# A trunk layer's attention mixers: the second logit pass over all 128 rows, and a compressed branch padded to 128 keys

## The chip, the cores and the metric

The kernel runs on one core of a Trainium2 chip. The metric is the device time of one execution in microseconds; of the kernel before it is the median of three runs. Engines are named as in the profile: PE is TensorE (PEld its weight loads), DVE VectorE, ACT ScalarE, POOL GpSimd, SP the engine whose queue issues most loads.

## What is computed

The reference is one layer of a decoder on 1024 tokens of 1024 features, in float32. After a first norm, four attention mixers work side by side, each with heads of 64 features: A (sparse attention with a selected, a window and a compressed branch, 4 heads), B (dilated windows in three groups, 2 heads each), C (forgetting attention, 4 heads) and D (latent attention, 4 heads). Their outputs are projected, gated and merged, and a gated MLP with a short convolution follows. Of mixer A, cut to what matters:

```python
lc = einsum('bqhd,bcd->bhqc', q_blk, kc) * scale          # compressed: 63 keys
p_c, _ = masked_softmax(lc, cmp_end <= t)
o_c = einsum('bhqc,bcd->bqhd', p_c, vc)
...
ls = einsum('bqhd,bqkd->bhqk', q_blk, ks) * scale + bias   # selected: here all keys up to t
lw = einsum('bqhd,bkd->bhqk', q_blk, kw) * scale + bias    # window: the last 512 keys
...
return g0 * o_c + g1 * o_s + g2 * o_w
```

## The kernel before

**Precision by passes.** Float32 products run as sums of float32r products: an operand x is split into hi = float32r(x) and lo = x - hi, and hi*hi + lo*hi + hi*lo is accumulated in PSUM. A head has 64 features, half of TensorE's 128 rows, so mixers A, B and C stack the halves: `q_pair` (L320) makes for each head e of a pair a tile qs[e] with q's hi part on the 64 partitions 64e.. and its lo part on the other 64; `k_pair` (L327) makes ks[e] with k's hi part on both. One pass over 128 rows then gives hi*hi + lo*hi, and a second pass over 64 rows adds q's hi times kl, k's lo part. `q_passes` (L443) lists these two. For the pairs of C and B, kl is one tile in which head e has the partitions 64e..; for A, whose keys all heads share (`shared`), the lo part already stands on both halves, as it does in KCL, the lo part of the compressed keys KC. Mixer D has operands of 96 rows and three passes.

**One softmax row block** (`softmax_rows`, L361): the passes of up to 512 keys into PSUM (L374; for B's groups 1 and 2 L372), one VectorE instruction that adds the bias and takes the running maximum into a tile P (L376), exp on ScalarE (L381), and scaling by the row sum and the branch's gate on VectorE (`normalize`). `pv` (L394) takes key blocks of 128 in groups of at most two: it transposes P's blocks for two query blocks on TensorE (L413), splits them on ScalarE (th, L419) and VectorE (tl, L420), zeroes the blocks that are masked throughout on GpSimd (L417, L418), and multiplies with the value stack: th with all 128 columns [hi | lo] (L428, L431), tl with the 64 of hi (L429). `fold` adds the two halves.

**Stages.** In program order: the norm and token-major columns, A's compressed keys and values (KC, KCL, VC; L484 to L595), D (about 150 to 275 us of the profile), A (275 to 516), C (516 to 640), B's group 0 (640 to 692), the projections of B's groups 1 and 2 (to 743.7) and their attention (to about 790), then the merge, the output projection and the MLP. A runs over 4 heads and in each over 4 pairs of query blocks (g): selected, window, compressed, each with its own P tiles, into one PSUM tile pvt. Queries' 128-row blocks take 12 key chunks a head over all keys, and as many in the window.

**Order.** The order of each engine's instructions is planned at build time: an instruction goes into its engine's queue by program order and readiness in the plan, and the queue is then strictly in order. So projections (`project`, 48 products of 512 columns each, L142 to L144 on tile pd) of the next mixers stand between the attention's products. `fill_tile` (L191) computes gate products early (tile pf) at the lowest priority; its weights come in two halves through the tile fraw. Tiles of one tag share a ring of BUFS[tag] buffers.

Of the kernel before, what the change touches and what calls it, by code (L numbers as in the profile page):

```python
"""Hybrid decoder trunk (one layer) on one Trainium2 core.

Normalisations run token-major; products take their operands feature-major (features on
partitions, tokens on the free axis), so normalised activations are transposed on TensorE.
Float32 products run as three float32r passes: an operand x is split exactly into
hi = float32r(x) and lo = x - hi, and hi*hi + hi*lo + lo*hi is accumulated in PSUM.
"""
# [16 lines left out]
D = 1024  # L24
# [13 lines left out]
BUFS = dict(qs=4, ks=4, kl=3, vs=2, vt=1, P=4, th=2, tl=2, bias=2, ot=2, fo=2, nm=8, lsq=1)  # L38
# [10 lines left out]
def shape_constants():  # L49
    """Arrays that depend on shapes alone."""  # L50
    c = {}
    # distance rows: [0,1280) dist = 1023 - i; [1280,1791) dist = 4 * (255 - i); [1792,1919) dist = 16 * (63 - i)
# [24 lines left out]
    # [open | causal triangle | closed] and, for the window's far end, [closed | triangle | open]  # L77
# [8 lines left out]
def body(tc, a, out):  # L86
# [39 lines left out]
    def load_weights(src, shape, pool_=None, scale=1.0, eng=None):  # L126
        """DMA one weight tile and split it into float32r halves."""
        pool_ = pool_ or wp
        raw = wp.tile([128] + shape, F32, name="wraw", tag="wraw", bufs=2)
        SP.dma_start(raw, src)  # L130
        hi = pool_.tile([128] + shape, F32R, name="whi", tag="whi", bufs=2)
        lo = pool_.tile([128] + shape, F32R, name="wlo", tag="wlo", bufs=2)
        split_weights(hi, lo, raw, eng or V, scale)
        return hi, lo

    def gemm(ps, lhs, rhs, kts, first=True, last=True):
        """ps += lhs^T rhs in three passes; lhs(kt) and rhs(kt) give (hi, lo)."""
# [8 lines left out]
    def row_rstd(rs, sums):  # L146
        """rs = 1 / sqrt(sums / D + eps), one per partition."""
        A.activation(rs, sums, AF.Sqrt, bias=epst[:, 0:1], scale=1.0 / D)
        V.reciprocal(rs, rs)
# [6 lines left out]
    def to_features(src, psum, dst, b):  # L156
        """dst (hi, lo) [128, KT, 512], token block b = transpose of src [128 tokens, D], split."""
# [17 lines left out]
    # ================= token mixers =================  # L175
    with ExitStack() as c1:
# [13 lines left out]
        # ---- gates that need nothing but h: work for TensorE whenever the mixers wait  # L190
        def fill_tile(i):  # L191
            br, m = FILL[i]
            w = []
            for ch in range(2):
                raw = ap.tile([128, 4, 128], F32, name="fraw", tag="fraw", bufs=2)
# [20 lines left out]
        # ---- h = rms_norm(x) * gain by token blocks, transposed and split  # L216
        def weights_tm(src):
            """Weights of the token-major columns, in four pieces of two feature tiles."""
# [31 lines left out]
        # ================= token-major columns: latents, rotary key, gates, forget logits =================  # L250
# [19 lines left out]
        cmpmask = ap.tile([128, 8, 64], F32, name="cmpmask")  # L270
        SP.dma_start(cmpmask, a["cmpmask"])
# [12 lines left out]
        def toeplitz(row):  # L284
            """tile[p, j]: row value at distance p + 896 - j."""
# [4 lines left out]
        def project(src, scale=1.0):  # L290
            """Feature-major projection of h: yields (half, psum tile)."""
# [9 lines left out]
        def permuted(ap_, hf, kind):  # L301
            """Columns of tokens 512*hf.. in natural, (r4,s,i) or (r4,4i+s) order, as [p, r4, s, i]."""
# [9 lines left out]
        def split(hi, lo, ps, kind):  # L312
            """hi = float32r(ps), lo = ps - hi."""
# [13 lines left out]
        def k_pair(src, kind="n", shared=False):  # L327
            ks = [ap.tile([128, S], F32R, name="ks", tag="ks", bufs=BUFS["ks"]) for _ in range(2)]
            kl = [ap.tile([128, S], F32R, name="kl", tag="kl", bufs=BUFS["kl"]) for _ in range(2 if shared else 1)]
            for hf, ps in project(src):  # L330
                for e in range(2):
# [7 lines left out]
                    else:  # L339
                        lo_of(permuted(kl[0][64 * e:64 * e + 64], hf, kind),  # L340
                              permuted(ks[e][64 * e:64 * e + 64], hf, kind), pe, kind)
            return ks, (kl if shared else [kl[0], kl[0]])
# [17 lines left out]
        # ---- one softmax row block: logits in chunks, joint maximum, exp, sum  # L360
        def softmax_rows(chunks, clamp=BIG, stat=None, two=False):  # L361
            """chunks: (passes, n, bias). Returns P [128, sum n] = exp(l - max) and its row sums;
            -max and the sums go to the columns of stat if there are any."""
            P = ap.tile([128, S], F32, name="P", tag="P", bufs=BUFS["P"])
# [29 lines left out]
        def pv(pvt, P2, blocks, first, last):  # L394
            """pvt[hi 64 | lo 64, 256 queries] += V^T P^T over key blocks. A block: the column of its
            first key in P for either query block (None where it is masked throughout), rows, V stack."""
# [3 lines left out]
            for bl in groups:  # L400
                kr = bl[0][1]
                # slots in an order that leaves the ones to move in one piece
# [30 lines left out]
        def fold(dst, pvt, e):  # L433
            """dst (partitions 64e..) = sum of the two halves of pvt."""
# [8 lines left out]
        def q_passes(qs, e, ks, kl, qb, k0, n):  # L443
            q = slice(128 * qb, 128 * qb + 128)
            r = slice(64 * e, 64 * e + 64)
            return [(qs[:, q], ks[:, k0:k0 + n], 0), (qs[r, q], kl[r, k0:k0 + n], 0)]

        def cuts(k0, k1):
            """Key chunks: at most 512 columns, none under 256 unless it is the only one."""
# [10 lines left out]
        def causal_blocks(vs, k1):  # L460
            """Key blocks of query blocks k1 - 2 and k1 - 1, both from key 0 on."""
            return [((128 * b, 128 * b), 128, vs[:, b]) for b in range(k1 - 1)] + [
                ((None, 128 * (k1 - 1)), 128, vs[:, k1 - 1])]
# [4 lines left out]
        def rotate(x, n):  # L468
            """x [128, n blocks, heads, 32] rotated in place; n = (first block, blocks, heads)."""
# [13 lines left out]
        # ================= A, compressed keys and values =================  # L483
        KC = ap.tile([128, 64], F32R, name="KC")  # L484
        KCL = ap.tile([128, 64], F32R, name="KCL")
        VC = ap.tile([64, 128], F32R, name="VC")
# [13 lines left out]
        # the keys' and the values' columns apart, zeros elsewhere: one product serves both  # L500
# [7 lines left out]
        # rms-normalised latents, transposed, gained and split  # L508
# [5 lines left out]
        for i, (c0, n, dst, gc) in enumerate(kinds):  # L514
            for b in range(8):
                sq = ap.tile([128, 256], F32, name="lsq", tag="lsq", bufs=BUFS["lsq"])
# [27 lines left out]
        # gates of A  # L544
# [3 lines left out]
        # log sigmoid(f + bias) = min(z, 0) - ln(1 + exp(-|z|)), then its running sum over tokens  # L548
# [28 lines left out]
        # gelu(x) = 0.5 x (1 + tanh(sqrt(2/pi) (x + 0.044715 x^3)))  # L577
# [19 lines left out]
        # ---- bias rows (table lookup by one-hot product), then to DRAM for the Toeplitz reads  # L597
# [12 lines left out]
        # Row copies at a pitch one (or four) longer than the one they are read at: each partition  # L610
        # then reads its row one (or four) further on.
# [5 lines left out]
        # ================= D: latent attention =================  # L617
# [25 lines left out]
        # on the partitions where the keys' tiles take it  # L643
# [18 lines left out]
        for pr in range(2):  # L662
            QD, KD = [], []
            for e in range(2):
# [5 lines left out]
                else:  # L670
                    # the two operands of a subtraction start in the same quadrant
# [34 lines left out]
        # ================= A: native sparse attention =================  # L706
        # n_sel equals the number of selected blocks at this sequence length, so every block is
        # selected whatever its importance, and the selected branch is causal attention over all keys.
        ks, kl = k_pair(a["win"][1], shared=True)
        va = v_pair(a["win"][2])  # L710
        for pr in range(2):
            qs = q_pair(a["win"][3 + pr])
            ot = new_ot()
            for e in range(2):
# [3 lines left out]
                for g in range(4):  # L718
                    pvt = new_pv()
                    # selected  # L720
# [605 lines left out]
```

## Time and profile before

| | |
|---|---|
| median of three runs | 1940.14 us (1940.08 to 1941.3) |
| the profiled execution, its span | 1942.8 us |
| granted TensorE clock, mean over the span | 0.992 |
| instructions | 24124 |

The trace is of one execution; its span is the time from its first to its last instruction and the only time that the profile gives for it, 2.7 us over the median of the runs. Clock 1.00 is 2.4 GHz. Products on TensorE overlap: in a timeline the start of one and its length are shown, and the end of one less the end of the one before it is what it adds to the engine's time. A form such as 64*128 64x256 is a product over 64 rows into 128 columns of outputs, with 256 moving columns.

### The profile page before, as it was taken

The page shows a single profiled execution, that of the slowest core. Times are in us where ns is not written, and L with a number is a line of the kernel's source. Part 1 is how long each engine was busy: PE and PEld are TensorE (multiplying, and loading weights), DVE is VectorE, ACT ScalarE, POOL GpSimd, SP SyncE. Part 2 cuts the span into 40 slices and gives each one's busy share as a digit, 9 for nine tenths or more (in the row PEclk, how much of TensorE's full clock was granted, in tenths as well). Part 3 has the DMA queues.
Part 4 walks back from the last instruction along what each step waited for, and adds up shares of the span by engine and source line. Part 5 has one row for each costly group of instructions (what it writes and reads, how often), then busy time and mean ns, then how long its engine had stood idle before and what let it go on. Part 6 is the DMA issues. An engine that isn't in the chain of part 4 may idle for free.

```text
span 1942.8 us, 24124 instructions
## 1 busy us (share of the span) xinstructions
PE 1890.3 (97%) x8894; PEld 1506.2 (78%) x8894; DVE 1103.0 (57%) x2109; ACT 789.6 (41%) x1466; POOL 513.0 (26%) x510
## 2 busy tenths in 40 slices
PE   7989999999999999999999999999999999999998
PEld 6767777676777777788888888778888888888786
DVE  4449867877777525432222245679777766733534
ACT  5436545554555534221212134444444444432432
POOL 3411111120120220011222200567676767100000
PEclk9999999999999999999999999999999999999999
DMA  7150110000001110321122232212222222354643
GB/s 252 41 149 17 62 45 24 24 31 20 28 22 43 51 44 28 124 74 53 59 69 65 69 125 108 98 56 98 76 87 76 87 77 82 114 157 147 222 156 109
DMA packets 55366, 158.83 MB, mean 82 GB/s; under 512 B 9344, under 2 KB 10704, under 8 KB 55248
## 3 DMA queue, kind: packets, MB, share of 16 engines
q1 hardware_dynamic: 42352, 124.09, 19.9%
q10 hardware_dynamic: 12896, 33.21, 4.9%
q8 instruction: 70, 1.15, 0.2%
q14 instruction: 48, 0.39, 0.1%
HBM read 129.91 MB, written 31.61 MB: 83 GB/s over the span
## 4 chain that ended last, share of the span: by engine, by line
PE 89%; DVE 4%; ACT 2%; issue 2%; DMA 1%; POOL 1%; ACTq 0%; DVEq 0%; SPq 0%; POOLq 0%
PE ps L374 6%; PE pgb L142 6%; PE pgb L143 6%; PE pgb L144 5%; PE pd L143 4%; PE pd L142 4%; PE pd L144 4%; PE pk L1217 4%; PE pk L1219 4%; PE pk L1218 4%; PE ptp L413 4%; PE pvt L428 2%; PE pvt L429 2%; PE py L143 2%; PE py L142 2%; PE pz L143 2%
## 5 line engine op out<-in xcount | busy, mean ns | idle before, releaser
L142 PE MATMUL pgb<-hh,whi 128*128 128x512 f32 x400 | 155.8, 390 | 1.0 <-ACT ft L206 0.7
L144 PE MATMUL pgb<-hh,wlo 128*128 128x512 f32 x400 | 155.6, 389 | 0.0
L143 PE MATMUL pgb<-hl,whi 128*128 128x512 f32 x400 | 155.6, 389 | 0.0
L120 DVE TENSOR_TENSOR wlo<-wraw,whi 128x1024 fp32r<-128x1024 f32 x25 | 30.6, 1224 | 210.3 <-ACT whi L119 210.3
L419 ACT CAST th<-ptp 128x512 fp32r<-128x512 f32 (+3 forms) x202 | 97.7, 517 | 118.8 <-PE ptp L413 108.5
L381 ACT ACTIVATE P<-P,nm 128x64 f32<-128x64 f32 (+8 forms) x160 | 107.8, 675 | 82.7 <-DVE nm L376 81.7
L420 DVE TENSOR_TENSOR tl<-ptp,th 128x512 fp32r<-128x512 f32 (+3 forms) x202 | 115.2, 598 | 35.9 <-ACT th L419 33.5
L142 PE MATMUL pd<-hh,whi 128*128 128x512 f32 x320 | 133.4, 417 | 1.9 <-DVE kl L318 1.9
L119 ACT CAST whi<-wraw 128x1024 fp32r<-128x1024 f32 x38 | 39.9, 1051 | 234.4 <-PE pgb L143 196.0
L143 PE MATMUL pd<-hl,whi 128*128 128x512 f32 x320 | 133.2, 416 | 0.0
L144 PE MATMUL pd<-hh,wlo 128*128 128x512 f32 x320 | 132.7, 415 | 0.0
L1217 PE MATMUL pk<-aset 128*128 128x512 f32 x320 | 124.6, 390 | 0.6 <-DVE y L1257 0.6
L1218 PE MATMUL pk<-aset 128*128 128x512 f32 x320 | 124.5, 390 | 0.5 <-DVE aset L120 0.5
L1219 PE MATMUL pk<-aset 128*128 128x512 f32 x320 | 124.4, 390 | 0.0
L1084 POOL TENSOR_TENSOR aset<-sums,aset 128x512 fp32r<-128x512 f32 x66 | 121.5, 1841 | 6.4 <-ACT aset L1083 6.4
L417 POOL MEMSET th<- 128x128 f32 x86 | 18.2, 212 | 377.5 <-PE pvt L428 233.7
L972 POOL TENSOR_TENSOR mg<-mg,tg 128x512 f32<-128x512 f32 x32 | 42.1, 1317 | 286.9 <-DVE tg L970 241.6
L413 PE MATMUL ptp<-miscc,P 128*128 128x128 f32 (+1 forms) x678 | 110.8, 274 | 2.9 <-DVE P L390 2.3
L1083 ACT CAST aset<-wraw 128x512 fp32r<-128x512 f32 x88 | 54.0, 617 | 97.9 <-PE pz L144 37.7
L120 DVE TENSOR_TENSOR aset<-at,aset 128x512 fp32r<-128x512 f32 x44 | 30.3, 691 | 107.2 <-ACT aset L119 107.0
L413 PEld LDWEIGHTS ptp<-miscc,P 128*128 128x128 f32 (+1 forms) x678 | 80.3, 139 | 14.0 <-DVE P L390 4.3
L1083 ACT CAST aset<-sums 128x512 fp32r<-128x512 f32 x66 | 40.8, 620 | 120.7 <-PE px L144 29.0
(359 smaller groups left out, 5129.4 us busy)
## 6 DMA issues: line engine op xcount, KB each, us to landing
wraw<-in_wup SPq DMA_DIRECT2D x44, 512.0 KB, 3.6
wraw<-in_wdn SPq DMA_DIRECT2D x44, 512.0 KB, 3.5
wraw<-in_wg SPq DMA_DIRECT2D x25, 512.0 KB, 3.6
act_d<-o ACTq DMA_DIRECT2D x22, 512.0 KB, 3.8
at<-act_d SPq DMA_DIRECT2D x44, 256.0 KB, 2.5
wraw<-in_win SPq DMA_DIRECT2D x20, 512.0 KB, 3.5
x<-in_x SPq DMA_DIRECT2D x8, 512.0 KB, 4.2
wraw<-in_wo SPq DMA_DIRECT2D x8, 512.0 KB, 5.0
```

The costliest lines, as they stand in the source:

```text
L142: T.matmul(ps, lh, rh, start=first and ii == 0, stop=False)
L143: T.matmul(ps, lh, rl, start=False, stop=False)
L144: T.matmul(ps, ll, rh, start=False, stop=last and ii == n - 1)
L374: T.matmul(ps[:, at:at + w], l, r, start=j == 0, stop=j == len(passes) - 1)
L381: A.activation(P[:, 0:c0], P[:, 0:c0], AF.Exp, bias=prev, scale=-1.0, accum_out=den)
L413: T.transpose(tp[0:kr, at[x]], P2[x[1]][:, c:c + kr], ident)
L419: A.copy(th[0:kr, i0:i1], tp[0:kr, i0:i1])
L420: V.tensor_tensor(tl[0:kr, i0:i1], tp[0:kr, i0:i1], th[0:kr, i0:i1].bitcast(F32), op=ALU.subtract)
L1084: eng.tensor_tensor(t[:, 1], src, t[:, 0].bitcast(F32), op=ALU.subtract)
L1217: T.matmul(ps[b][:, w], ah[:, c], wh[:, w], start=st, stop=False)
L1218: T.matmul(ps[b][:, w], ah[:, c], wl[:, w], start=False, stop=False)
L1219: T.matmul(ps[b][:, w], al[:, c], wh[:, w], start=False, stop=sp)
```

## The change

The second pass runs over all 128 rows: q's stack [hi, lo] times a kl that has k's lo part on both halves, which adds lo*lo to the sum. For the unshared keys kl becomes two tiles, and GpSimd copies each head's 64 partitions to the other 64. Mixer A's compressed and window softmaxes share one P tile (columns 0 to 63 and from 64 on); the compressed block is taken with 128 keys, of which the last 64 meet zeros in VC, ahead of the window's blocks. Room is made by one buffer less for fraw, a mask in bfloat16, and squares in another tag's ring. Comments are left out of the diff.

```diff
-BUFS = dict(qs=4, ks=4, kl=3, vs=2, vt=1, P=4, th=2, tl=2, bias=2, ot=2, fo=2, nm=8, lsq=1)
+BUFS = dict(qs=4, ks=4, kl=4, vs=2, vt=1, P=4, th=2, tl=2, bias=2, ot=2, fo=2, nm=8)
...
-                raw = ap.tile([128, 4, 128], F32, name="fraw", tag="fraw", bufs=2)
+                raw = ap.tile([128, 4, 128], F32, name="fraw", tag="fraw", bufs=1)
...
-        cmpmask = ap.tile([128, 8, 64], F32, name="cmpmask")
-        SP.dma_start(cmpmask, a["cmpmask"])
+        cmf = ap.tile([128, 8, 64], F32, name="cmf", tag="th", bufs=BUFS["th"])
+        SP.dma_start(cmf, a["cmpmask"])
+        cmpmask = ap.tile([128, 8, 64], BF16, name="cmpmask")
+        V.tensor_copy(cmpmask, cmf)
...
         def k_pair(src, kind="n", shared=False):
-            kl = [ap.tile([128, S], F32R, name="kl", tag="kl", bufs=BUFS["kl"]) for _ in range(2 if shared else 1)]
+            kl = [ap.tile([128, S], F32R, name="kl", tag="kl", bufs=BUFS["kl"]) for _ in range(2)]
...
-                        lo_of(permuted(kl[0][64 * e:64 * e + 64], hf, kind),
+                        lo_of(permuted(kl[e][64 * e:64 * e + 64], hf, kind),
                               permuted(ks[e][64 * e:64 * e + 64], hf, kind), pe, kind)
-            return ks, (kl if shared else [kl[0], kl[0]])
+            if not shared:
+                for e in range(2):
+                    o = 64 - 64 * e
+                    G.tensor_copy(kl[e][o:o + 64], kl[e][64 * e:64 * e + 64].bitcast(F32))
+            return ks, kl
...
-        def softmax_rows(chunks, clamp=BIG, stat=None, two=False):
-            P = ap.tile([128, S], F32, name="P", tag="P", bufs=BUFS["P"])
+        def softmax_rows(chunks, clamp=BIG, stat=None, two=False, into=None):
+            P = ap.tile([128, S], F32, name="P", tag="P", bufs=BUFS["P"]) if into is None else into
...
-        def q_passes(qs, e, ks, kl, qb, k0, n):
+        def q_passes(qs, ks, kl, qb, k0, n):
             q = slice(128 * qb, 128 * qb + 128)
-            r = slice(64 * e, 64 * e + 64)
-            return [(qs[:, q], ks[:, k0:k0 + n], 0), (qs[r, q], kl[r, k0:k0 + n], 0)]
+            return [(qs[:, q], ks[:, k0:k0 + n], 0), (qs[:, q], kl[:, k0:k0 + n], 0)]
...
-        def causal_blocks(vs, k1):
+        def causal_blocks(vs, k1, at=0):
-            return [((128 * b, 128 * b), 128, vs[:, b]) for b in range(k1 - 1)] + [
-                ((None, 128 * (k1 - 1)), 128, vs[:, k1 - 1])]
+            return [((at + 128 * b, at + 128 * b), 128, vs[:, b]) for b in range(k1 - 1)] + [
+                ((None, at + 128 * (k1 - 1)), 128, vs[:, k1 - 1])]
...
-        VC = ap.tile([64, 128], F32R, name="VC")
+        VC = ap.tile([128, 128], F32R, name="VC")
...
-                sq = ap.tile([128, 256], F32, name="lsq", tag="lsq", bufs=BUFS["lsq"])
+                sq = ap.tile([128, 256], F32, name="lsq", tag="fo", bufs=BUFS["fo"])
...
                     for qb in (2 * g, 2 * g + 1):
+                        P = ap.tile([128, S], F32, name="P", tag="P", bufs=BUFS["P"])
                         ch = causal_chunks(mk, qb, max(0, 128 * qb - 512), 128 * qb + 128, bias)
                         if qb >= 4:
                             ch[0][0].insert(1, (idb, wmask[:, 128:384], 0))
-                        P, n, den, nm = softmax_rows(ch)
-                        normalize(P, n, den, nm, gate[:, qb, 3 * h + 2:3 * h + 3])
+                        W, n, den, nm = softmax_rows(ch, into=P[:, 64:S])
+                        normalize(W, n, den, nm, gate[:, qb, 3 * h + 2:3 * h + 3])
+                        W, n, den, nm = softmax_rows(
+                            [(q_passes(qs[e], KC, KCL, qb, 0, 64), 64, cmpmask[:, qb])], clamp=CLAMP, into=P[:, 0:64])
+                        normalize(W, n, den, nm, gate[:, qb, 3 * h:3 * h + 1], guard=True)
                         P2.append(P)
                     if g < 2:
-                        bl = causal_blocks(va[:, 1], 2 * g + 2)
+                        bl = causal_blocks(va[:, 1], 2 * g + 2, 64)
                     else:
                         k0 = 2 * g - 4
-                        bl = [((128 * i if i < 5 else None, 128 * (i - 1) if i else None), 128, va[:, 1, k0 + i])
+                        bl = [((64 + 128 * i if i < 5 else None, 64 + 128 * (i - 1) if i else None), 128, va[:, 1, k0 + i])
                               for i in range(6)]
-                    pv(pvt, P2, bl, False, False)
-                    # compressed
-                    P2 = []
-                    for qb in (2 * g, 2 * g + 1):
-                        P, n, den, nm = softmax_rows(
-                            [(q_passes(qs[e], e, KC, KCL, qb, 0, 64), 64, cmpmask[:, qb])], clamp=CLAMP)
-                        normalize(P, n, den, nm, gate[:, qb, 3 * h:3 * h + 1], guard=True)
-                        P2.append(P)
-                    pv(pvt, P2, [((0, 0), 64, VC)], False, True)
+                    pv(pvt, P2, [((0, 0), 128, VC)] + bl, False, True)
```

## Rows read from the trace of the kernel before

**Rows 1.** Page, part 1: busy time, share of the span, instructions

```profile
PE 1890.3 (97%) x8894; PEld 1506.2 (78%) x8894; DVE 1103.0 (57%) x2109; ACT 789.6 (41%) x1466; POOL 513.0 (26%) x510
```

**Rows 2.** Busy time by stage, in the columns PE, PEld, DVE, ACT, POOL

```profile
150.00:250.00 100.00, 96.36 (x562) 78.10 (x563) 87.71 (x235) 60.09 (x125) 15.98 (x32) 0.98 0.11 38
275.00:516.00 241.00, 239.31 (x1216) 169.69 (x1215) 183.02 (x620) 128.33 (x322) 36.76 (x88) 0.99 0.08 25
516.00:640.00 124.00, 123.91 (x662) 89.64 (x661) 90.70 (x247) 66.51 (x137) 16.39 (x39) 1.00 0.09 32
640.00:692.00 52.00, 47.53 (x235) 36.44 (x234) 27.12 (x75) 27.10 (x63) 14.23 (x29) 1.00 0.17 54
...
743.70:780.00 36.30, 36.29 (x186) 26.22 (x184) 23.84 (x55) 20.69 (x46) 0.00 (x0) 1.00 0.06 22
```

**Rows 3.** TensorE's timeline in mixer B's groups 1 and 2: start, length

```profile
750.77 1.03 PE L413 MATMUL ptp<-miscc,P 128*128 128x128 f32 x8
...
752.26 0.28 PE L372 MATMUL ps<-ks,qs 128*128 128x256 f32 x1
752.47 0.38 PE L372 MATMUL ps<-kl,qs 64*128 64x256 f32 x1
...
754.66 0.51 PE L142 MATMUL pf<-hh,fh 128*128 128x512 f32 x1
755.00 0.28 PE L429 MATMUL pvt<-tl,vs 128*64 128x256 f32 x1
755.12 0.28 PE L428 MATMUL pvt<-th,vs 128*128 128x256 f32 x1
```

**Rows 4.** TensorE's timeline in mixer D

```profile
239.81 0.39 PE L142 MATMUL pd<-hh,whi 128*128 128x512 f32 x1
240.04 0.89 PE L374 MATMUL ps<-kd,qd 96*128 96x512 f32 x3
```

**Rows 5.** The logit lines L374 and L372: count, ns min/median/max, forms

```profile
L374 PE MATMUL ps<-kl,qs x160: 379/436/502, 275.5 to 671.7; 64*128 64x256 f32 x72, 64*128 64x384 f32 x44, 64*128 64x512 f32 x44
...
L374 PE MATMUL ps<-KCL,qs x32: 293/294/421, 278.4 to 504.7; 64*128 64x64 f32 x32
...
L372 PE MATMUL ps<-kl,qs x32: 379/381/384, 743.9 to 778.7; 64*128 64x256 f32 x32
```

**Rows 6.** TensorE's timeline in mixer A, a compressed logit row

```profile
308.54 0.19 PE L374 MATMUL ps<-KC,qs 128*128 128x64 f32 x1
308.66 0.29 PE L374 MATMUL ps<-KCL,qs 64*128 64x64 f32 x1
308.89 0.39 PE L428 MATMUL pvt<-th,vs 128*128 128x256 f32 x1
```

**Rows 7.** TensorE's timeline in mixer A, the compressed value products

```profile
302.04 0.40 PE L144 MATMUL pd<-hh,wlo 128*128 128x512 f32 x1
302.36 0.33 PE L429 MATMUL pvt<-tl,VC 64*64 64x256 f32 x1
302.53 0.27 PE L431 MATMUL pvt<-th,VC 64*128 64x256 f32 x1
302.74 0.50 PE L142 MATMUL pd<-hh,whi 128*128 128x512 f32 x1
```

**Rows 8.** Groups of instructions of GpSimd: count, busy us, mean ns

```profile
L123 POOL TENSOR_SCALAR wraw<-wraw 128x1024 f32<-128x1024 f32 x7 | 19.4, 2776 | 22.3 <-ACT whi L122 13.1 <-PE ps L374 9.2
...
L120 POOL TENSOR_TENSOR fl<-fraw,fh 128x512 fp32r<-128x512 f32 x14 | 18.6, 1334 | 128.4 <-ACT fh L119 110.2 <-DMA rsb<-in_rowmask 14.0 <-DMA rows_d<-rsb 3.3
...
L502 POOL MEMSET blk<- 128x2048 f32 x2 | 3.6, 1808 | 7.9 <-PE pd L143 7.9
```

**Rows 9.** DMA issues: KB each, us to landing

```profile
fraw<-in_wg SPq DMA_DIRECT2D x14, 256.0 KB, 2.9
```

**Rows 10.** Chain that ended last, end of mixer B's group 0

```profile
675.15 1.06 ACT ks L334
676.24 1.08 DVE kl L318
```

More of the change, by code (lines that the diff above doesn't have):

```diff
@@ L721, in body @@
                     P2 = []
-                    mk = lambda qb_, kk, n: q_passes(qs[e], e, ks[0], kl[0], qb_, kk, n)
+                    mk = lambda qb_, kk, n: q_passes(qs[e], ks[0], kl[0], qb_, kk, n)
                     for qb in (2 * g, 2 * g + 1):
@@ L729, in body @@
                     P2 = []
-                    mk = lambda qb_, kk, n: q_passes(qs[e], e, ks[1], kl[1], qb_, kk, n)
+                    mk = lambda qb_, kk, n: q_passes(qs[e], ks[1], kl[1], qb_, kk, n)
                     for qb in (2 * g, 2 * g + 1):
+                        P = ap.tile([128, S], F32, name="P", tag="P", bufs=BUFS["P"])
                         ch = causal_chunks(mk, qb, max(0, 128 * qb - 512), 128 * qb + 128, bias)
@@ L777, in body @@
                         for kk, n in cuts(0, 128 * qb + 128):
-                            ps_ = q_passes(qs[e], e, ks[e], kl[e], qb, kk, max(n, 256))
+                            ps_ = q_passes(qs[e], ks[e], kl[e], qb, kk, max(n, 256))
                             if kk + n == 128 * qb + 128:
@@ L804, in body @@
                 P2 = []
-                mk = lambda qb_, kk, n: q_passes(qs[e], e, ks[e], kl[e], qb_, kk, n)
+                mk = lambda qb_, kk, n: q_passes(qs[e], ks[e], kl[e], qb_, kk, n)
                 for qb in (2 * g, 2 * g + 1):
@@ L839, in body @@
                     for at, qq, kk, ll in ((0, qs1, ks1, kl1), (256, qs2, ks2, kl2)):
-                        ps_ += [(l, r, at) for l, r, _ in q_passes(qq[e], e, kk[e], ll[e], qb, 256 * r4, 256)]
+                        ps_ += [(l, r, at) for l, r, _ in q_passes(qq[e], kk[e], ll[e], qb, 256 * r4, 256)]
                     P, n, den, nm = softmax_rows([(ps_, 512, bt[:, st])], stat=(st1[:, qb, e, 0:1], st1[:, qb, e, 1:2]),
```

## The prediction

> **What bounds the kernel now.** I read the page's busy shares first, then a table by stage, then TensorE's own timeline. The page has TensorE busy for 97% of the span, VectorE 57%, ScalarE 41% and GpSimd 26% [rows 1]. The table by stage says where the change lies: mixer A's attention (275 to 516 us), C's (516 to 640), B's group 0 (640 to 692) and B's groups 1 and 2 (743.7 to 780). TensorE is busy 99% of A and all of C [rows 2]. VectorE is the second engine everywhere: 183 of A's 241 us, 91 of C's 124. So a TensorE microsecond saved there is real until VectorE, or the chain of one softmax row through VectorE, ScalarE and back, becomes the limit.
>
> Busy TensorE is not useful TensorE, so the timeline comes next. I read it by the ends of successive products, since starts overlap. In a run of logit passes, eight products follow the first one, whose end is 752.26 + 0.28 = 752.54; the last, a 512-column product, ends at 754.66 + 0.51 = 755.17 [rows 3]. That is 2.63 us. At the pace of two neighbouring 256-column products (0.12 us from 755.00 to 755.12) and of a 512-column one (0.23 us, from 239.81 to 240.04 in [rows 4]) they need 7 x 0.12 + 0.23 = 1.07. The other 1.56 us belong to eight changes between products over 64 rows and over 128 rows: 0.195 us each, so **0.39 us for each 64-row pass**, once in, once out. What changes is the row count and nothing else: the three 96-row passes of mixer D end 240.93 - 240.20 = 0.73 us after the product before them, 0.24 each, the price of 512 columns [rows 4].
>
> **The change, part by part.**
>
> *Second logit pass over 128 rows (lines 443 to 446).* The instruction count stays. The passes concerned are 160 + 32 over kl and 32 over KCL [rows 5]. By the loops, A has 4 heads x 24 = 96 and the 32 over KCL, C 4 x 12 = 48, B's group 0 16, B's groups 1 and 2 32. A KCL pass has 64 columns: its end comes 0.22 us after KC's (308.73 to 308.95), where a product with its own weight load takes at least 0.11 (eight transposes, 1.03 us together with a tail of 0.28: 0.75 / 7, [rows 3]); the next 256-column product ends 0.33 later instead of 0.12 [rows 6]. So 0.11 + 0.21 = 0.32 each. TensorE gets back:
> A 96 x 0.39 + 32 x 0.32 = 47.6; C 48 x 0.39 = 18.7; B group 0 16 x 0.39 = 6.2; B groups 1 and 2 32 x 0.39 = 12.5 us.
>
> *Compressed branch padded to 128 keys.* The two VC products of each of A's 16 query pairs stand over 64 rows. Ends: 302.44, 302.69, 302.80, then 303.24 for the next projection product [rows 7]: 0.25 instead of 0.12, 0.11, and 0.44 instead of 0.23. That is 0.34 each, 5.4 us in all. Transposes, casts and subtractions of that block keep their number and columns. P tiles fall from six to four a query pair, with four buffers; that removes waits if anything, but the compressed softmax now stands ahead of the window's products. I take zero: the projections for later stages stand between.
>
> The total is 90 us of TensorE time: 53 in A, 37 in C and B.
>
> *What of it comes through.* With 53 us gone, A's TensorE work is 239.3 - 53 = 186 us beside VectorE's unchanged 183: neither can be 99% busy. The nearest row for two engines so matched is mixer D's, 150 to 250 us, with the same softmax and no 64-row pass: VectorE reaches 0.877, TensorE 0.964 [rows 2]. I use D's shares as what each engine can reach.
> A: 183.0 / 0.877 = 208.7 (TensorE would allow 193): 32 saved, and 20 lost to VectorE.
> C: TensorE (123.9 - 18.7) / 0.964 = 109.1, VectorE 103.4: 15 saved.
> B groups 1 and 2: VectorE 23.84 / 0.877 = 27.2, TensorE 23.8: 9 of 36.3 saved.
> B group 0: TensorE already waits for 4.5 of 52 us, for key copies and VectorE's low parts at its end [rows 10]; I take 5 of 6.2.
> Sum 61 us. Bounds: in A VectorE at 95% gives 193 (48 saved) and below that the whole 53; at the poor end the order, planned before the run, may leave TensorE idle for another 12 us (20 saved).
>
> *The keys' low parts (k_pair).* Each of the five unshared pairs gets two GpSimd copies of 64 x 1024, ten in all. No such copy is in the trace. From below the memset of 128 x 2048 gives half of 1.81, 0.9 us; from above the scaling of 128 x 1024 takes 2.78 [rows 8]. I take 2.7, since it reads as the scaling does: 27 us of GpSimd, which is 15% busy in A and 13% in C. The copy waits for VectorE's subtraction of the projection's second half. Behind it in GpSimd's queue stand the zero fills of masked blocks, on which the value products wait, and the next weights' scaling and split. The cover is the query and value projections between a pair's keys and its first logits, 48 products x 2 x 0.23 = 22 us. I charge 2 us in all; without cover, 10 x 2.8 = 28.
>
> *One fraw buffer, four kl, bf16 mask, squares in the fo tag.* With one fraw buffer a gate tile's second half is loaded only after the first is split: 2.9 to land [rows 9] and 1.33 to subtract [rows 8]. On SP's queue that load now waits for GpSimd, and later weights wait behind it. Seven tiles x 4.2 = 30 us at worst, nothing where other products run; these are the lowest in priority, so I take zero. Four kl buffers, two a pair, give the keys' low parts the rotation that ks has already: no new wait. The mask's conversion is one VectorE instruction before A, under projections; the squares gain a second buffer.
>
> Taken together: 61 - 2 = 59. The profiled execution spans 1942.8 us, 2.7 over the 1940.1 of the runs; 1942.8 - 59 = 1883.8, and a median of **1881**.
>
> **A rule that speaks against it.** In this order 64-row passes stand singly between 128-row products, and each costs more than a 128-row one [rows 3]. The Trainium skill, TensorEngine Tiling (Performance Considerations, When to Use Tiling), counsels the reverse for contractions of 64: two row tiles side by side, up to twice as fast. By it a filled pass would cost twice a half-filled one: as an estimate 224 x 0.07 (half of the 0.14 of a mean pass at the paces above) = 16 us more, 1956. The same page (Tiling Modes, Key Properties) says that a change of tiling mode drains the engine, and counts halved columns as a mode too; the trace agrees for rows, but not for columns, as the 128*64 product at 755.00 and the 128*128 at 755.12 follow at 0.12 us.
>
> **The rivals.**
> 1. *TensorE stays the bound throughout*: all 90 us come back, 1850; with VectorE at 95%, some 1857. For it: projections and gates lie ready as filler in every stage. Against: D, with filler too, does not reach it. Chance 0.2.
> 2. *The softmax chain binds earlier*: A gives 20, C 10, B 9; less 4 for copies and zero fills, 35: 1905. For it: the window's products now wait for both compressed softmaxes as well, and VectorE's 24% of idle time in A shows how often a row's chain keeps it waiting. Chance 0.2.
> 3. *GpSimd's queue becomes the wait* (slower): copies planned ahead of the next projection's weights hold them until the second half's keys are out: four key copies on ScalarE, 4 x 1.06 [rows 10], the subtraction 1.1, two copies 5.6, then scaling 2.8 and split 2.7 (twice the 1.33 of half the columns): 16.4 us, five times 82, against the 61 gained: 1940 + 21 = 1961. It decides from 12.2 us a pair on. Against: weights are double-buffered and split well ahead of their products; GpSimd has idle time. Chance 0.03.
> 4. *The price does not follow the rows* (the change does not do what it says): the pass costs 0.39 for another reason, such as loading the same queries twice, and the time stays at 1940. Against: projections load the same weights twice at 0.23. Chance 0.02.
> 5. *Half-filled passes were the cheap ones*, the arithmetic being 224 more halves: 1956. Against: the spacing above. Chance 0.01.
>
> **How the numbers follow.** The forecast, 1866 to 1896, has 0.54; rivals 1 and 2 have 0.2 each, which the range takes in down to about VectorE at 95% and up to 1905: 1855 to 1906; some 0.15 is left out. Faster (by over 0.2%, 3.9 us, about what can be told from no change): forecast and rivals 1 and 2, 0.94; same 0.02 (rival 4); slower 0.04 (rivals 3 and 5).
>
> **What would show it.** Right: passes over kl and KCL read 128*128 and end 0.12 us after their neighbour at 256 columns; no product on VC stands over 64 rows; A's stage is some 209 us with VectorE at about 88% and short TensorE gaps that VectorE or transposes end; C is near 109. Wrong: second passes still 0.31 apart (rival 4); TensorE waiting for wlo or zero fills, with GpSimd's copies ahead of them (rival 3); A above 220 us with VectorE under 83% (rival 2) or under 197 with TensorE at 97% (rival 1). Stages from 830 us on should keep their lengths.

## The result, and the profile after

| | before | after |
|---|---|---|
| median of 4 runs each, same chip | 1940.72 us (1940.08 to 1944.46) | **1879.51 us** (1877.05 to 1880.98) |
| ratio, 95% interval | 1 | **0.9678** [0.9665, 0.9691] |
| span of the profiled execution | 1942.8 us | 1879.2 us |

The change saves 61.2 us in the medians and 63.6 in the two traces. Wherever the record has both, the span is 1.8 or 1.9 us shorter than the time of its own run; by that the traced execution before took some 1944.6 us, 4 over the median, and the traced one after took 1881.0, 1.5 over it, and the difference of 2.4 us lies there. The forecast was 1881, in a range of 1855 to 1906. The page's first part after, beside [rows 1]: TensorE does as many products as before, in 73 us less, and VectorE's time falls by only 11.

```profile
PE 1817.5 (97%) x8894; PEld 1489.8 (79%) x8894; DVE 1092.4 (58%) x2110; ACT 789.7 (42%) x1467; POOL 527.6 (28%) x520
```

For the comparison each stage is cut where its last output store is issued, and B's groups 1 and 2 (B12 below) begin with their first biased softmax row on VectorE. Busy time by stage, columns as in [rows 2], before: A, C, B's group 0 with the projections behind it, B12, and the merge to the end.

```profile
263.40:517.20 253.80, 252.11 (x1280) 180.44 (x1279) 186.62 (x626) 132.52 (x329) 42.02 (x90) 0.99 0.08 28
517.20:641.30 124.10, 124.01 (x658) 89.58 (x658) 90.99 (x247) 66.64 (x138) 17.61 (x38) 1.00 0.09 32
641.30:745.00 103.70, 98.92 (x456) 78.23 (x454) 36.27 (x87) 44.44 (x88) 22.90 (x33) 0.98 0.16 48
745.00:799.50 54.50, 52.73 (x280) 39.72 (x281) 36.81 (x84) 25.09 (x57) 2.58 (x2) 1.00 0.09 25
799.50:1942.00 1142.50, 1123.40 (x4954) 923.28 (x4952) 587.28 (x672) 386.77 (x571) 366.09 (x273) 0.99 0.31 101
```

The same stages after; the last row is the stretch that answers to A in [rows 2].

```profile
262.90:477.20 214.30, 208.77 (x1278) 170.65 (x1277) 183.25 (x626) 131.71 (x330) 49.84 (x96) 1.00 0.10 34
477.20:588.40 111.20, 108.94 (x652) 85.43 (x651) 93.05 (x247) 66.30 (x138) 19.44 (x39) 1.00 0.10 35
588.40:686.80 98.40, 93.58 (x457) 76.61 (x456) 35.87 (x86) 43.70 (x87) 27.09 (x38) 0.98 0.16 50
686.80:733.70 46.90, 43.63 (x286) 37.00 (x286) 37.46 (x84) 25.31 (x58) 2.58 (x2) 1.00 0.11 30
733.70:1879.00 1145.30, 1125.59 (x4960) 925.14 (x4958) 578.07 (x672) 387.47 (x571) 369.05 (x273) 0.99 0.31 101
...
275.00:476.00 201.00, 195.47 (x1211) 159.51 (x1210) 179.64 (x620) 127.40 (x322) 44.65 (x94) 1.00 0.09 31
```

Saved: A 39.5 us, C 12.9, B's group 0 with the projections 5.3, B12 7.6. The sum is 65.3; the rest of the program is 1.7 longer (the last rows above stop 0.8 and 0.2 us short of the spans' ends, so from the merge on it is 2.2 longer, and 0.5 shorter ahead of A). A has as many products as before (1278 and 1280), so its 39.5 are not work put off. In the last row VectorE is busy 0.894 of the stretch and TensorE 0.97, against 0.759 and 0.99 before.

TensorE's timeline in B12 after, beside [rows 3]: the kl passes read 128*128, and successive passes end 0.117 us apart (from 692.18 + 0.28 = 692.46 to 692.53 + 0.28 = 692.81 is 0.35 for three), entering and leaving kl alike.

```profile
692.18 0.28 PE L378 MATMUL ps<-kl,qs 128*128 128x256 f32 x1
692.30 0.28 PE L378 MATMUL ps<-ks,qs 128*128 128x256 f32 x1
692.41 0.28 PE L378 MATMUL ps<-kl,qs 128*128 128x256 f32 x1
692.53 0.28 PE L378 MATMUL ps<-ks,qs 128*128 128x256 f32 x1
```

A compressed row and a product on VC in mixer A after, beside [rows 6, 7]: KCL's pass ends 0.12 us after KC's (277.13 and 277.01), where it was 0.22, and VC's tl product 0.11 after its neighbour (286.71 and 286.60), where it was 0.25.

```profile
276.82 0.19 PE L380 MATMUL ps<-KC,qs 128*128 128x64 f32 x1
276.85 0.28 PE L380 MATMUL ps<-KCL,qs 128*128 128x64 f32 x1
...
286.20 0.40 PE L143 MATMUL pd<-hl,whi 128*128 128x512 f32 x1
286.43 0.28 PE L435 MATMUL pvt<-tl,VC 128*64 128x256 f32 x1
```

What TensorE's weight loads wait for in A after (line waited for, us in total, times, longest; these waits overlap products in part):

```profile
PEld pvt L434 <- ACT th L425: 10.0, 34, 0.4
PEld ptp L419 <- DVE P L398: 4.7, 9, 1.9
PEld ps L380 <- DVE nm L382: 4.2, 17, 0.7
PEld pvt L435 <- POOL tl L424: 2.7, 3, 2.1
```

Below, TensorE's "lost" time in a stage is its length less the products' time at the paces of undisturbed neighbours, summed over all records of the stage: 0.11 us up to 128 columns, 0.117 for 256, 0.18 for 384, 0.23 for 512. In A the products need 196 us in both kernels; 57 were lost before, 18 after. In B12 it was 14.8 and is 5.8.

The gate products that fill_tile puts into gaps stand elsewhere, too. Those alone (TensorE's windows of tile pf: busy, count), first of before, then of after, in A, in B12, and from there on:

```profile
263.40:517.20 253.80, 19.83 (x55) 0.99 0.08 28
745.00:799.50 54.50, 20.93 (x68) 1.00 0.09 25
799.50:1942.00 1142.50, 4.08 (x18) 0.99 0.31 101
```

```profile
262.90:477.20 214.30, 14.88 (x43) 1.00 0.10 34
686.80:733.70 46.90, 21.60 (x74) 1.00 0.11 30
733.70:1879.00 1145.30, 5.48 (x24) 0.99 0.31 101
```

Twelve of them, 12 x 0.23 = 2.8 us of TensorE, have left A: six are done in B12 and six behind it.

### The profile page after: what moved, and what is told of

Its sections match the earlier page's. It is cut to its first block, busy times and chain, and to the rows that moved or that the text cites. A ratio compares the mean times of both kernels' runs of the same rounds, so it can differ in the third digit from the quotient of the medians.

```text
span 1879.2 us, 24134 instructions
## 1 busy us (share of the span) xinstructions
PE 1817.5 (97%) x8894; PEld 1489.8 (79%) x8894; DVE 1092.4 (58%) x2110; ACT 789.7 (42%) x1467; POOL 527.6 (28%) x520
## 4 chain that ended last, share of the span: by engine, by line
PE 68%; DVE 3%; DMA 1%; ACT 1%; issue 1%; POOL 0%; SPq 0%; DVEq 0%; ACTq 0%; POOLq 0%
PE pgb L142 6%; PE pgb L143 6%; PE pgb L144 6%; PE pk L1219 4%; PE pk L1221 4%; PE pk L1220 4%; PE py L143 2%; PE py L142 2%; PE pz L143 2%; PE pz L142 2%; PE py L144 2%; PE pz L144 2%; PE px L143 2%; PE px L142 2%; PE px L144 2%; PE pd L142 2%
## 5 line engine op out<-in xcount | busy, mean ns | idle before, releaser
L142 PE MATMUL pgb<-hh,whi 128*128 128x512 f32 x400 | 155.8, 390 | 1.1 <-ACT ft L206 0.7
L387 ACT ACTIVATE P<-P,nm 128x512 f32<-128x512 f32 (+7 forms) x160 | 108.1, 677 | 64.6 <-DVE nm L382 63.4
L1086 POOL TENSOR_TENSOR aset<-sums,aset 128x512 fp32r<-128x512 f32 x66 | 131.2, 1988 | 5.3 <-ACT aset L1085 5.2
L142 PE MATMUL pd<-hh,whi 128*128 128x512 f32 x320 | 129.9, 406 | 2.1 <-DVE kl L320 2.0
L143 PE MATMUL pd<-hl,whi 128*128 128x512 f32 x320 | 129.0, 403 | 0.0
L419 PE MATMUL ptp<-miscc,P 128*128 128x128 f32 x678 | 112.2, 274 | 5.9 <-DVE P L396 3.1
L423 POOL MEMSET th<- 128x128 f32 x86 | 18.9, 220 | 291.2 <-PE pvt L434 130.7
L419 PEld LDWEIGHTS ptp<-miscc,P 128*128 128x128 f32 x678 | 80.4, 140 | 15.5 <-DVE P L396 4.9
```

Source lines behind the costliest of these rows:

```text
L142: T.matmul(ps, lh, rh, start=first and ii == 0, stop=False)
L143: T.matmul(ps, lh, rl, start=False, stop=False)
L387: A.activation(P[:, 0:c0], P[:, 0:c0], AF.Exp, bias=prev, scale=-1.0, accum_out=den)
L419: T.transpose(tp[0:kr, at[x]], P2[x[1]][:, c:c + kr], ident)
L1086: eng.tensor_tensor(t[:, 1], src, t[:, 0].bitcast(F32), op=ALU.subtract)
```

## The experiments

Every ratio is to the kernel before, run on the same chip beside it. e5 to e8 ran on another chip than the rest; the kernel before took 1941.8 us there and 1940.7 to 1942.4 beside the others. A difference "over after" is one of medians and holds to about 1 us.

**Is the price on the change of height?** *e4_side_by_side*: the kernel before, with B12's order of passes changed so that equal heights stand together.

```diff
+                    ps_ = [ps_[0], ps_[1], ps_[3], ps_[2]]
```

> The kernel before, but in mixer B's groups 1 and 2 the order of the four passes of a row is hi, lo, lo, hi instead of hi, lo, hi, lo: as many passes over 64 rows, two of them side by side. Theory (the price belongs to the change of height): 16 rows x 2 changes x 0.195 = 6.2 us less of TensorE, 4 to 6 us faster than before; a 64-row pass after another 64-row pass ends 0.12 us after it. Rival (every 64-row pass is slow by itself, as one loaded without overlap would be): no change, and the second of the two ends 0.31 us after the first.

1937.4 us, 0.9973 [0.9964, 0.9982], 4.7 faster; B12 takes 48.5 us instead of 54.5. Its TensorE timeline (x2 is two products in one row):

```profile
746.40 0.36 PE L372 MATMUL ps<-ks,qs 128*128 128x256 f32 x1
746.70 0.50 PE L372 MATMUL ps<-kl,qs 64*128 64x256 f32 x2
747.12 0.51 PE L372 MATMUL ps<-ks,qs 128*128 128x256 f32 x2
747.56 0.50 PE L372 MATMUL ps<-kl,qs 64*128 64x256 f32 x2
```

Ends are at 746.76, 747.20, 747.63 and 748.06: each two products take 0.43 or 0.44 us, two paces of 0.12 and one change of 0.195. The second of two 64-row passes is as cheap as a 128-row one. So the price belongs to the change of height, as it was expected. Half the changes gone give 32 x 0.195 = 6.2 us; TensorE's lost time fell by 6.1.

*e3_c_half*: the kernel after, with only C's 48 second passes back over 64 rows.

```diff
-            return [(qs[:, q], ks[:, k0:k0 + n], 0), (qs[:, q], kl[:, k0:k0 + n], 0)]
+            return [(qs[:, q], ks[:, k0:k0 + n], 0), (qs[r, q], kl[r, k0:k0 + n], 0)]
```

> The changed kernel with mixer C's 48 second passes over 64 rows again; the copies of kl stay, and C leaves out q's lo part times k's lo part as before. Theory: TensorE takes 48 x 0.39 = 18.7 us more in C and is its bound again; C goes from 111 to about 124 us, the kernel to 1890 to 1895 us. Rival (the gain came from other edits: buffers, P tiles): within 2 us of the changed kernel.

1892.04 us, 0.9741 [0.9725, 0.9758]: 12.5 over after. Its windows row of C, and a pass in its timeline:

```profile
478.40:601.80 123.40, 122.88 (x652) 88.45 (x651) 93.58 (x247) 66.73 (x138) 19.29 (x39) 1.00 0.09 32
```

```profile
519.87 0.33 PE L380 MATMUL ps<-ks,qs 128*128 128x384 f32 x1
520.14 0.44 PE L380 MATMUL ps<-kl,qs 64*128 64x384 f32 x1
520.50 0.38 PE L434 MATMUL pvt<-th,vs 128*128 128x256 f32 x1
```

C is back at 123.4 us. Ends at 520.20, 520.58 and 520.88 are 0.38 and 0.30 apart where the paces are 0.18 and 0.12: 0.38 us for a pass. This part can be switched on and off by itself, and with nothing else moved: in the two traces all 8894 products of TensorE, and the instructions of VectorE, ScalarE and GpSimd, stand in the same order. So the planned order does not depend on the height of the passes.

**Which half of the change pays?** *e1_passes_only*: the kernel after with the compressed branch as before (its own P tiles, VC over 64 rows).

```diff
-        VC = ap.tile([128, 128], F32R, name="VC")
+        VC = ap.tile([64, 128], F32R, name="VC")
...
-                    pv(pvt, P2, [((0, 0), 128, VC)] + bl, False, True)
+                    pv(pvt, P2, bl, False, False)
...
+                    pv(pvt, P2, [((0, 0), 64, VC)], False, True)
```

> The changed kernel with mixer A's compressed branch as it was: P tiles of its own, VC over 64 rows, its products last. Theory (each change between products over 64 and over 128 rows costs TensorE 0.195 us, and A is then held by VectorE and the softmax chain): the 16 pairs of VC products take 5.4 us of TensorE again, in a stage where TensorE has idle time; 0 to 5 us slower than the changed kernel, 1880 to 1885 us. Rival (the shared P tile, with four instead of six tiles a query pair, is what shortens A): 1890 us or more.

1877.34 us, 0.9666 [0.9652, 0.9681]: no slower than after; the intervals overlap. Set beside before, it shows the passes by themselves, since the traces have TensorE's products from A to the end of B12 in the same order, but for five: A goes from 253.8 to 218.5 us, 35.3 less, where the forecast's prices, 96 x 0.39 + 32 x 0.32, give 47.7, and the rest to the end of B12 from 282.3 to 250.6. *e2_pad_only* is the other half by itself: the kernel before with the padded, shared block.

```diff
-        VC = ap.tile([64, 128], F32R, name="VC")
+        VC = ap.tile([128, 128], F32R, name="VC")
...
-                    pv(pvt, P2, [((0, 0), 64, VC)], False, True)
+                    pv(pvt, P2, [((0, 0), 128, VC)] + bl, False, True)
```

> The kernel before with the compressed branch alone changed (one P tile with the window's, VC with 128 keys); the second logit passes stay over 64 rows. Theory: A is held by TensorE there, so the 5.4 us come back nearly whole: 4 to 6 us faster than before, 1934 to 1937 us. Rival (the shared P tile is what shortens A): 15 us faster or more. Rival (the price does not follow the rows): no change.

1945.61 us, 1.0018 [1.0008, 1.0027]: slower by some 3.5 us, where 4 to 6 us faster was expected. Windows of e1 (A, B12), then of e2 (A, B12), and then e2's gate products in A and behind B12:

```profile
263.00:481.50 218.50, 214.52 (x1285) 171.67 (x1284) 186.91 (x627) 131.45 (x330) 46.21 (x94) 1.00 0.09 33
...
688.30:732.10 43.80, 41.91 (x280) 35.81 (x280) 36.31 (x84) 25.16 (x58) 2.57 (x2) 1.00 0.13 38
```

```profile
263.40:514.90 251.50, 247.06 (x1275) 181.04 (x1274) 188.95 (x626) 132.22 (x330) 43.67 (x92) 0.99 0.08 29
740.30:796.70 56.40, 53.78 (x284) 40.48 (x284) 38.08 (x84) 24.63 (x56) 2.56 (x2) 1.00 0.07 20
```

```profile
263.40:514.90 251.50, 15.93 (x43) 0.99 0.08 29
...
796.70:1946.00 1149.30, 6.20 (x26) 0.99 0.30 101
```

The padding shortens A, by 4.2 us on top of the passes (218.5 to 214.3) and by 2.3 alone. But in both pairs A takes 43 gate products instead of 55, and B12 is longer by 3.1 and 1.9. In e2 the part behind B12 is longer too, by 6.4 us to the spans' ends: it has 26 gate products instead of 18 (1.8 us), and one wait there, of TensorE for VectorE's merge (`PE pgb L142 <- DVE mg L963`), is 2.4 us where the same wait is 0.3 in the kernel before. The 61 us are the passes', with e1's small edits (the mask, the squares' ring, the fourth kl buffer), which no run has alone; the padding gives back later what it saves in A, and no gain of it is shown.

**The copies and fraw.** *e8_zero_half*: the kernel after, with the other half of each kl set to zero instead of copied. It leaves out lo*lo in C and B.

```diff
-                    G.tensor_copy(kl[e][o:o + 64], kl[e][64 * e:64 * e + 64].bitcast(F32))
+                    G.memset(kl[e][o:o + 64].bitcast(F32), 0.0)
```

> The changed kernel with the other half of each unshared kl tile set to zero by GpSimd instead of copied, so that k's low part times q's low part is left out in C and B: the ten GpSimd instructions remain, but wait for no projection. Theory (the copies are hidden): within 2 us of the changed kernel. Rival (GpSimd's queue waits behind the copies and others wait for it): 3 us faster or more.

1876.89 us, 0.9676 [0.966, 0.9692], no difference from after. The ten copies after and the ten zero fills here, from the groups of GpSimd:

```profile
L347 POOL CAST kl<-kl 64x1024 fp32r<-64x1024 f32 x10 | 10.6, 1064 | 13.3 <-DVE kl L320 11.2 <-DVE nm L394 1.9
```

```profile
L347 POOL MEMSET kl<- 64x1024 f32 x10 | 9.7, 965 | 13.6 <-PE ps L380 13.4
```

A copy takes 1.06 us and waits for VectorE's subtraction. The zero fill occupies GpSimd nearly as long, so what this run takes away is that wait, and it costs nothing. The occupancy was not taken away, so it is not shown that the copies as such are free.

*e11_passes_zero* has e1's and e8's edits together.

> Mixer A's compressed branch as before the change, the second passes over 128 rows, and the other half of each unshared kl set to zero instead of copied (k's low part times q's low part is left out there). Theory (padding bought nothing, copies cost next to nothing): 1873 to 1878 us, at least as fast as the changed kernel. Rival (the padding pays once the copies no longer hold GpSimd's queue): 1879 us or more.

1878.06 us, 0.967 [0.9655, 0.9684]. After, e1, e8 and e11 lie between 1876.9 and 1879.5 with overlapping intervals; none is shown to beat after.

*e9_one_fraw_before*: the kernel before with one fraw buffer.

```diff
-                raw = ap.tile([128, 4, 128], F32, name="fraw", tag="fraw", bufs=2)
+                raw = ap.tile([128, 4, 128], F32, name="fraw", tag="fraw", bufs=1)
```

> The kernel before with one fraw buffer instead of two. Theory (the second half's load is hidden, as gate products are the last in priority): within 3 us of before. Rival (loads behind it on SP's queue come late): 5 us slower or more.

1941.6 us, 0.9995 [0.9985, 1.0005]: no difference to within 3 us.

**What holds A now?** *e5_vec_more*: the kernel after with 64 more VectorE instructions of 0.41 us, one behind each selected and each window row of A, on constants into fold's scratch tile. *e6_vec_more_before*: the same in the kernel before.

```diff
+                        tmp = ap.tile([128, 256], F32, name="fo", tag="fo", bufs=BUFS["fo"])
+                        V.tensor_tensor(tmp, miscc[:, 0:256], miscc[:, 128:384], op=ALU.add)
```

> The changed kernel with one more VectorE instruction behind each selected and each window row of mixer A, 64 in all: a sum of two constants of 128x256 into scratch that nothing reads, some 0.35 us, 22 us in all. Theory (VectorE holds A after the change): A grows from 214 us by most of it, 15 to 22 us; 1893 to 1901 us. Rival (TensorE still holds A, or the latency of a row's chain does, and VectorE has 31 us to spare): under 8 us; 1880 to 1887 us.

> The kernel before with the same 64 VectorE instructions in mixer A. Theory (there TensorE holds A, and VectorE idles for 67 of 254 us): 0 to 6 us slower than before, 1941 to 1948 us. Rival (VectorE was on the path already): 12 us or more.

e5: 1886.93 us, 0.972 [0.9706, 0.9735], 7.4 over after. e6: 1956.76 us, 1.0081 [1.0066, 1.0097], 15 over before, where 0 to 6 was expected. Windows of A and B12 in e5, then in e6, and the gate products of e5 in the same two:

```profile
262.30:499.80 237.50, 230.00 (x1366) 185.33 (x1366) 205.02 (x689) 134.12 (x334) 50.40 (x98) 1.00 0.10 35
706.20:747.70 41.50, 32.98 (x221) 27.80 (x220) 35.96 (x84) 22.60 (x54) 0.00 (x0) 0.90 0.09 20
```

```profile
264.70:541.40 276.70, 273.55 (x1364) 195.98 (x1363) 212.44 (x689) 135.95 (x335) 45.78 (x92) 0.99 0.08 30
770.30:818.30 48.00, 40.41 (x217) 30.04 (x218) 36.28 (x84) 22.68 (x52) 0.00 (x0) 0.93 0.06 12
```

```profile
262.30:499.80 237.50, 43.45 (x133) 1.00 0.10 35
706.20:747.70 41.50, 1.97 (x6) 0.90 0.09 20
```

After, A grows by 23 us for 22 more of VectorE. But so it does before (253.8 to 276.7 for 26 more), where TensorE was busy 99%. In both, A now holds 80 to 90 more gate products (133 for 43 in e5; 139 for 55 in e6), 84 to 90 x 0.23 = 19 to 21 us, and TensorE's lost time in A hardly moves (18.3 to 21.1; 57.3 to 60.9). The order is planned with the added instructions in it, and the plan itself puts that work into A, which would have come later. So A's growth is mainly its gate products' time, before and after alike, and neither run shows what holds A when the order stays as it is. The bill comes in B12, whose filler is used up: it gets shorter (46.9 to 41.5 us), but its lost time rises from 5.8 to 15.5 and from 14.8 to 22.7, and its granted clock falls to 0.90 and 0.93, which is (1 - 0.90) x 41.5 x 2 = 8.3 us at 1.2 GHz in e5.

*e12_five_gates*: the kernel after with five gate tiles computed early instead of seven, to take B12's filler away without touching A.

```diff
-NFILL = 7
+NFILL = 5
```

> The changed kernel with five gate tiles computed early instead of seven, so 96 products (22 us) go from the mixers to the merge. Theory (gate products fill gaps that would be empty otherwise): mixer A within 4 us of its length, B's groups 1 and 2 lose 8 to 12 us of TensorE time instead of 6, and the kernel is 6 to 14 us slower. Rival (TensorE's work is the bound throughout, wherever it stands): within 3 us.

1885.33 us, 0.9705 [0.969, 0.9719], 5.8 over after. A, B12 and a stretch at B12's end, and the gate products of B12:

```profile
261.90:475.30 213.40, 207.94 (x1276) 170.35 (x1275) 183.30 (x626) 130.49 (x328) 47.16 (x94) 1.00 0.09 31
683.30:725.20 41.90, 32.61 (x217) 27.21 (x216) 36.20 (x84) 22.29 (x53) 0.00 (x0) 0.92 0.06 14
717.00:722.00 5.00, 3.12 (x14) 2.68 (x15) 3.66 (x11) 0.01 (x1) 0.00 (x0) 0.50 0.00 0
```

```profile
683.30:725.20 41.90, 0.00 (x0) 0.92 0.06 14
```

A is as it was. B12 without filler is the same 42 us at nearly the same low clock as in e5, with 16.8 us lost, more than the 8 to 12 expected, while the kernel lost a little less than the 6 to 14. The mechanism of e5's bill is shown by itself. The stretch at the end shows the clock: TensorE stands idle for 3.6 us until 718.9, in a wait for VectorE; the granted clock falls to 0.50 (1.2 GHz) within that wait and is back at 1.00 by 724.

*e7_vec_less*: the kernel after with fold's copy on ScalarE instead of VectorE (64 copies in the program, 16 of them in A).

```diff
-            V.tensor_copy(tmp[o_], pvt[s_])
+            A.copy(tmp[o_], pvt[s_])
```

> The changed kernel with the first instruction of each fold, a copy of 64x256 out of PSUM of 0.42 us, on ScalarE instead of VectorE: 16 in A, 48 or so in all, 7 us of VectorE in A and 20 in all. Theory (VectorE holds A and shares C and B's last part): 5 to 12 us faster than the changed kernel, 1867 to 1875 us. Rival (chain latency or TensorE): within 3 us, 1877 to 1882.

1885.23 us, 0.971 [0.9693, 0.9726]: 5.7 slower, where 5 to 12 faster was expected. A is longer with less of VectorE. Its window, and one of the two longest waits of TensorE in it, with what GpSimd did just before:

```profile
259.80:485.40 225.60, 216.09 (x1299) 177.02 (x1298) 178.60 (x610) 136.50 (x346) 47.48 (x96) 0.98 0.09 32
```

```profile
310.06 2.34 POOL L124 TENSOR_TENSOR wlo<-wraw,whi 128x1024 fp32r<-128x1024 f32 x1
...
312.60 0.39 PE L434 MATMUL pvt<-th,vs 128*128 128x256 f32 x1 [2.29 <-POOL th L423]
```

Of the 11.3 us that A is longer, some 5 are work: the new order has 331 projection products (tile pd) in A where after has 309, and C with B's group 0 is 3.8 us shorter. Another 4.9 are two waits of 2.3 and 2.6 us for a zero fill (L423) that stands in GpSimd's queue behind a weight's scaling and split, the second ending at 416.2; behind each the clock is at 1.2 GHz for 3.4 us. After has one such wait in A, of 1.85 us. So the run does not show what less VectorE does for A with the order unchanged, only that taking 16 copies, 6.7 us, off it brought nothing. Whether the copy's place in ScalarE's queue, in front of the single pvt buffer, costs time too is not shown: a second pvt buffer was not tried.

*e10_scalar_more*: the kernel after with 128 more ScalarE copies of 128 x 128, meant for A.

```diff
+                        A.copy(u, ident)
+                        A.copy(u, ident)
```

> The changed kernel with two more ScalarE instructions behind each selected and each window row of mixer A, 128 copies of a 128x128 constant into scratch, some 0.27 us each, 34 us in all; ScalarE is 61% busy in A, so none of it lacks room. Theory left over from the prediction (VectorE's throughput holds A): within 3 us of the changed kernel. Theory after the last runs (A follows the chain of a row through all three engines as the order was planned; gate products move into the gaps, and the time is TensorE's work plus the gaps that nothing fills): A grows by 10 us or more, more gate products stand in it, and the kernel is 3 to 10 us slower.

1881.84 us, 0.9687 [0.9671, 0.9703]. The experiment did not do what it was meant to. The last of ScalarE's four groups of copies into u (count, ns, first and last start):

```profile
L751 ACT COPY u<-miscc x32: 281/299/311, 101.5 to 220.5; 128x128 f32<-128x128 f32 x32
```

The copies depend on nothing in A, and the plan put them all between 99.9 and 220.5 us, into the stages ahead of A. So A's unchanged 215.3 us says nothing about ScalarE. (In e5 the instructions, in the scratch ring that fold shares, did stand in A, from 261 to 489 us.) Whether more ScalarE work would lengthen A stays open.

## Why the prediction was right, and where not

*The price of a 64-row pass* (0.39 us, in and out of another height) is shown by e3, e4 and the spacing after. Rivals 4 and 5 fall (rival 5's mean pass is 0.15 us at the forecast's own paces, not 0.14, which makes 17 us of its 16). By the Trainium skill, TensorEngine Tiling (Tiling Modes, Key Properties), a change of tiling mode drains the engine; the runs fit that where the rows of a product change (0.195 us a change). Products of 64 and of 128 columns of outputs go on at 0.12 us; the forecast took that for a mode change without a drain, but no row tells in which mode a product ran. The page's counsel of two row tiles side by side for contractions of 64 was not tried: e4's neighbours stand on the same 64 rows. What the runs show is that where such products stand singly, full rows are cheaper by the whole price.

*A, 32 saved of 53.* Measured 39.5, with nearly equal product counts: 13.5 of the 53 did not come through where some 20 were taken. The stretch has the length that D's share of VectorE gave within 4% (201 for 209; VectorE 0.894 for 0.877), but as a saving that is 40 for 32. So rival 1, all 53, and rival 2, 20, are both wrong for A.

*The reason given for it is the weak step*: that VectorE's busy share, taken from D, sets A's length, "a TensorE microsecond saved there is real until VectorE, or the chain of one softmax row ..., becomes the limit". No run bears out the share: e7 took 6.7 us off VectorE in A and A did not get shorter, and in after TensorE itself is still busy 97% of A. By that reason VectorE had 24% of slack in A before, and e6 should have cost little; in A TensorE's lost time did rise by 3.6 us only, and the 15 us of the program came mostly with the gate products that the plan moved. So part of the closeness in A is luck. What is shown: the order of the queues is the same with 64-row and with 128-row passes (e1 and before, e3 and after), so the height changes were paid on top of it, and their removal shows until the order's own waits are bare. Of the 57 us lost in A before, 53 were height changes by the forecast's prices; of the 18 lost after, most must be new. The weight loads' waits there are for ScalarE's th, for VectorE's P and nm and for zero fills, steps of a softmax row's chain, which the same sentence of the forecast names. How much each of them makes of the 18 us stays open.

*C, 15 saved*: 12.9, and e3 gives 12.2 back. *B's group 0, 5*: 5.3. *B12, 9*: 7.6, with six more gate products in it (74 for 68).

*The padding term, 5.4 us of TensorE in A*, was mis-sized for the program: e1 runs without it at no loss, and e2 alone is 3.5 us slower. A's gain of 4.2 is there, but 2.8 of it are the twelve displaced gate products, and B12 and the part behind it take it back. The failing step is that TensorE time saved in A was added up as time saved in the program, without asking what had filled A's gaps and where it would go.

*The copies, 2 us.* Each was put at 2.7 by the nearest scaling and takes 1.06, nearest to the lower end of the bounds (0.9). Rival 3's 16.4 us a pair would have been some 13; no wait behind a copy appeared (the two waits of TensorE for a zero fill, 1.85 us in A and 0.9 in C, stand behind a weight's scaling). *One fraw buffer, zero*: e9 shows no difference, in the kernel before.

*The total.* 61 - 2 = 59 predicted, 61.2 in the medians, 63.6 in the spans. By stages: A 7.5 better than forecast, C and B12 3.5 worse together, so the errors cancel in part. Stages from the merge on should have kept their lengths; they are 2.2 us longer (1143.3 to 1145.5 to the spans' ends), with six more gate products (1.4 us).

## What to carry to other kernels

Read TensorE's timeline by the ends of successive products, and compare each form with its neighbours: where two heights alternate, a half-filled product of 256 columns can cost four times a full one (0.12 + 0.39 us for 0.12), and filling it with zeros or a harmless term takes that away; grouping equal heights takes part of it away (half in e4). A saving in one stage of a planned order is judged by the whole program: work of low priority that filled the stage moves on, and a later stage may lack it or have to carry it. An added load that shall test a stage must be tied to that stage, and the trace must show that it stayed there.

## What the runs showed of the hardware that was not expected

A 64-row product right after another 64-row product adds 0.12 us at 256 columns, no more than a 128-row one, and the change costs the same 0.195 in either direction (e4: groups of two end 0.43 and 0.44 apart). A GpSimd copy of 64 x 1024 from one half of the partitions to the other, rounded to float32r on the way, takes 1.06 us, 0.1 more than a zero fill of the same size (0.965). With its gate products gone, B12 ran at a mean granted clock of 0.90 to 0.93 in three kernels (e5, e6, e12) and at 1.00 in after; in all three TensorE stands idle there for 3.6 us, waiting for VectorE's `wx`, which the transposes at B12's end read, and for 1.4 in after. The 16 transposes behind that wait take 3.84 us in e12, at a clock of 0.50, where eight take 1.03 at 1.00 [rows 3].
